# im2col on one core: all plane copies on VectorE, and loads without a descriptor limit

## The chip, the cores and the metric

The kernel runs on 1 core of one Trainium2 chip. The metric is the device time in microseconds (us) of one execution; lower is better. The time before is a median of three runs.

## The reference

The function is im2col with a 3 x 3 window, no padding and stride 1. The input `x` is float32 of shape (16, 64, 32, 32). For each of the 16 x 64 = 1024 image planes and each of the 9 offsets (ki, kj) of the window, the output holds the 30 x 30 subplane that begins at (ki, kj):

```python
h_out = h - kernel_size + 1          # 30
w_out = w - kernel_size + 1          # 30
cols = np.zeros((batch, c * kernel_size * kernel_size, h_out * w_out), dtype=np.float32)
...
            patch = x[b, :, i:i + kernel_size, j:j + kernel_size].copy()
            cols[b, :, col_idx] = patch.ravel()
```

There is no arithmetic in it. 4.19 MB are read, and nine shifted copies of nearly each plane, 33.18 MB, are written.

## The kernel before

The 1024 planes are spread over 128 partitions, 8 planes on each (`CPP` = 8). In DRAM the 8 planes of a partition are 32 KB in one piece (`x_v`), and the 72 output planes that come of them are one piece too (`out_v`). So each load and each store moves, for each of 128 partitions, one long row.

The whole input fits in one buffer, `in_tile`. It is loaded in three pieces, all issued from SyncE's queue (SP) by the helper `load` (L33 to L39): image rows 0 to 32 (plane 0, 4 KB per partition), rows 32 to 200 (the `bulk`, 21 KB per partition) and rows 200 to 256 (7 KB per partition). The helper passes `max_dma_last_dim=7168`, which cuts a row longer than 7168 bytes into descriptors of that size: the bulk becomes 3 descriptors for each partition. The other two loads have rows of 4096 and 7168 bytes and stay whole.

Output planes are built in `out_tile`, which holds two input planes' worth of output (2 x 9 x 900 floats per partition) and has two buffers. The loop at L49 goes over c = 0, 2, 4, 6. For each of the two planes (`s`) and each offset (`kk`) one instruction copies a 30 x 30 window, strided in `in_tile`, to 900 contiguous elements of `out_tile`; that makes 72 copies. The tuple `on_act` (L47) deals them out in turn: of every five copies the second and the fourth go to ScalarE (L57), the rest to VectorE (L59), in all 29 and 43.

Stores are issued from SP too, in the order of the loop. For c = 0 there is one store per plane (L62, 32400 bytes per partition each); for c = 2, 4 and 6 one store per pair of planes (L77, 64800 bytes per partition each). The first store is made to wait, besides its copies, for the bulk load (the manual dependency at L68). As `out_tile` has two buffers, the copies of c = 4 wait until both stores of c = 0 have landed, and those of c = 6 until the store of c = 2 has. The order on each engine is the order of the code (`manual_schedule`). After compilation the first load is moved into the program's first block, ahead of the opening barrier (L94 to L107).

Of the kernel before, what the change touches and what calls it, by code (L numbers as in the profile page):

```python
# [1 line left out]

# [3 lines left out]


def _im2col(ctx, tc, x, K, out):


    nc = tc.nc
    P = nc.NUM_PARTITIONS

    B, C, H, W = x.shape
    HO = H - K + 1
    WO = W - K + 1
    KK = K * K
    assert out.shape == (B, C * KK, HO * WO)
    CPP = B * C // P
    assert CPP * P == B * C and C % CPP == 0 and CPP % 4 == 0  # L20

    x_v = x.rearrange("b (cp c2) h w -> (b cp) (c2 h w)", c2=CPP)
    out_v = out.rearrange("b (cp c2 kk) n -> (b cp) c2 (kk n)", c2=CPP, kk=KK)

    in_pool = ctx.enter_context(tc.tile_pool(name="in_pool", bufs=1))
    out_pool = ctx.enter_context(tc.tile_pool(name="out_pool", bufs=2))

    ctx.enter_context(tc.manual_schedule())

    in_tile = in_pool.tile([P, CPP, H, W], x.dtype, name="in_tile")  # L30
    in_flat = in_tile.rearrange("p c h w -> p (c h w)")

    def load(queue, r0, r1):  # L33

        return queue.dma_start(
            out=in_flat[:, r0 * W : r1 * W],
            in_=x_v[:, r0 * W : r1 * W],
            max_dma_last_dim=7168,
        )  # L39

    cuts = [0, H, 200, CPP * H]
    first = load(nc.sync, cuts[0], cuts[1])
    bulk = load(nc.sync, cuts[1], cuts[2])
    load(nc.sync, cuts[2], cuts[3])


    on_act = (False, True, False, True, False)  # L47
    n = 0
    for c in range(0, CPP, 2):  # L49
        out_tile = out_pool.tile([P, 2, KK, HO, WO], x.dtype, name="out_tile")  # L50
        for s in range(2):
            for kk in range(KK):
                ki, kj = divmod(kk, K)
                src = in_tile[:, c + s, ki : ki + HO, kj : kj + WO]
                dst = out_tile[:, s, kk]
                if on_act[n % len(on_act)]:
                    nc.scalar.copy(out=dst, in_=src)  # L57
                else:
                    nc.vector.tensor_copy(out=dst, in_=src)  # L59
                n += 1  # L60
            if c == 0:
                st = nc.sync.dma_start(  # L62
                    out=out_v[:, s],
                    in_=out_tile[:, s].rearrange("p kk i j -> p (kk i j)"),
                )
                if s == 0:

                    tc.add_manual_dep(  # L68
                        st.ins,
                        bulk.ins.name,  # L70
                        mybir.DependencyInfo(
                            mybir.DependencyClass.Sync, mybir.DependencyReason.DATA
                        ),
                        reason="the store follows the bulk of the loads",
                    )
        if c > 0:
            nc.sync.dma_start(  # L77
                out=out_v[:, c : c + 2].rearrange("p c n -> p (c n)"),
                in_=out_tile.rearrange("p c kk i j -> p (c kk i j)"),
            )  # L80
    return first


def kernel(
    tc: tile.TileContext,
    x: bass.AP,
    kernel_size: bass.AP,
    out: bass.AP,
):
    with ExitStack() as ctx:  # L90
        first = _im2col(ctx, tc, x, int(kernel_size), out)


    tc.close()  # L94
    tc.compile()  # L95
    blocks = tc.nc.main_func.blocks
    load = first.ins
    home = next(b for b in blocks if any(i.name == load.name for i in b.instructions))
    home.instructions = [i for i in home.instructions if i.name != load.name]
    head = list(blocks[0].instructions)  # L100
    at = next(
        k
        for k, i in enumerate(head)
        if i.engine == load.engine and type(i).__name__ == "InstDrain"
    )
    head.insert(at, load)
    blocks[0].instructions = head  # L107


# [1 line left out]
_INS = ['x', 'kernel_size']  # L111
_OUTS = [((16, 576, 900), 'float32')]

_NUMBERS = {'kernel_size': 3}


# [26 lines left out]
```

## Time and profile before

| what | value |
|---|---|
| median of three runs | 91.66 us (91.61 to 92.06) |
| the profiled execution's own time | 91.61 us |
| its span, first to last instruction | 89.8 us |
| VectorE (DVE) busy | 23.5 us, 43 copies |
| ScalarE (ACT) busy | 26.2 us, 29 copies and one table load |
| DMA | 1408 packets, 37.37 MB, busy for 97.2% of 16 engines' span |
| HBM read, written | 4.19 MB, 33.18 MB |

The profile is of one execution. Busy time of an engine is the time in which at least one of its instructions is recorded as running, so overlapping records count once. A DMA packet is one descriptor's work on one of the core's 16 DMA engines. In the answers by stretches of time a packet's bytes and time are put down to the stretch in which it began; so over a stretch shorter than some packets the DMA share can read above 1, and 0 in the next. TensorE has no work here.

### The profile page before, as it was taken

The numbers are of one execution on the slowest core, as the hardware profiler recorded it, in microseconds if no ns is written. First come the engines' busy times: TensorE is split into PE (matmuls) and PEld (weight loads), VectorE is DVE, ScalarE is ACT, GpSimd is POOL, SyncE is SP. The second block draws the span as 40 slices with busy tenths as digits, with TensorE's granted clock in tenths as the row PEclk, the third lists the DMA queues.
The fourth block names the chain that finished last, engine by engine and source line by source line (L and its number), as shares of the span: only waits on it lengthen the run. The fifth ranks groups of instructions, "written<-read, shape, count | busy, mean of one in ns | idle before, by whom it ended". The sixth has DMA issues, their size and how long they took to land.

```text
span 89.8 us, 140 instructions
## 1 busy us (share of the span) xinstructions
DVE 23.5 (26%) x43; ACT 26.2 (29%) x30; POOL 0.2 (0%) x4
## 2 busy tenths in 40 slices
DVE  0380499960000089500000399300000000000000
ACT  5391499930000089910000399300000000000000
POOL 0000000000000000000000000000000000000000
DMA  4999999998899999875999999999999997689990
GB/s 106 428 440 425 418 513 462 462 447 375 361 433 462 693 462 462 375 317 260 433 462 462 462 462 462 462 462 462 462 462 462 462 404 317 289 375 462 462 462 0
DMA packets 1408, 37.37 MB, mean 416 GB/s; under 512 B 128, under 2 KB 128, under 8 KB 768
## 3 DMA queue, kind: packets, MB, share of 16 engines
q1 hardware_dynamic: 1408, 37.37, 97.2%
HBM read 4.19 MB, written 33.18 MB: 416 GB/s over the span
## 4 chain that ended last, share of the span: by engine, by line
DMA 45%; DVE 16%; DVEq 1%; issue 0%; SPq 0%
DMA out_dram<-out_tile 35%; DVE out_tile L59 16%; DMA in_tile<-in_x_dram 10%; DVEq L95 1%; DVEq L59 0%; SPq L77 0%
## 5 line engine op out<-in xcount | busy, mean ns | idle before, releaser
L57 ACT COPY out_tile<-in_tile 128x900 f32<-128x900 f32 x29 | 24.9, 939 | 29.9 <-DMA out_dram<-out_tile 25.3
L59 DVE COPY out_tile<-in_tile 128x900 f32<-128x900 f32 x43 | 23.5, 623 | 33.4 <-DMA out_dram<-out_tile 26.0
L57 ACT ACT_TABLE_LOAD x1 | 1.3, 1283 | 0.8 <-PEq L124 0.8
L124 POOL MEMSET const-bfloat16-1.0<- 128x1 bf16 x1 | 0.1, 102 | 0.0
L124 POOL MEMSET const-uint8-127<- 128x1 uint8 x1 | 0.1, 101 | 0.0
L124 POOL MEMSET const-float32-0.0<- 128x1 f32 x1 | 0.1, 99 | 0.2 <-issue 0.2
L124 POOL MEMSET const-float32-1.0<- 128x1 f32 x1 | 0.1, 98 | 0.0
## 6 DMA issues: line engine op xcount, KB each, us to landing
out_dram<-out_tile SPq DMA_DIRECT2D x3, 8100.0 KB, 31.3
out_dram<-out_tile SPq DMA_DIRECT2D x2, 4050.0 KB, 14.9
in_tile<-in_x_dram SPq DMA_DIRECT2D x1, 2688.0 KB, 9.3
in_tile<-in_x_dram SPq DMA_DIRECT2D x1, 896.0 KB, 11.0
in_tile<-in_x_dram SPq DMA_DIRECT2D x1, 512.0 KB, 3.6
```

Source lines behind the costliest of these rows:

```text
L57: nc.scalar.copy(out=dst, in_=src)
L59: nc.vector.tensor_copy(out=dst, in_=src)
L95: tc.compile()
L124: nc = _bacc.Bacc("TRN2", target_bir_lowering=False, num_devices=1)
```

## The change

Two things change. The helper `load` no longer limits the size of a descriptor, so that the bulk load's 21504 bytes per partition need not be cut. And all 72 copies become `nc.vector.tensor_copy`: `on_act` and its counter go, and no instruction of the kernel's own is left on ScalarE. The stores, the cuts of the loads, the buffers and the manual dependency stay as they are.

```diff
     def load(queue, r0, r1):
 
         return queue.dma_start(
-            out=in_flat[:, r0 * W : r1 * W],
-            in_=x_v[:, r0 * W : r1 * W],
-            max_dma_last_dim=7168,
+            out=in_flat[:, r0 * W : r1 * W], in_=x_v[:, r0 * W : r1 * W]
         )
...
-
-    on_act = (False, True, False, True, False)
-    n = 0
     for c in range(0, CPP, 2):
         out_tile = out_pool.tile([P, 2, KK, HO, WO], x.dtype, name="out_tile")
         for s in range(2):
             for kk in range(KK):
                 ki, kj = divmod(kk, K)
-                src = in_tile[:, c + s, ki : ki + HO, kj : kj + WO]
-                dst = out_tile[:, s, kk]
-                if on_act[n % len(on_act)]:
-                    nc.scalar.copy(out=dst, in_=src)
-                else:
-                    nc.vector.tensor_copy(out=dst, in_=src)
-                n += 1
+                nc.vector.tensor_copy(
+                    out=out_tile[:, s, kk],
+                    in_=in_tile[:, c + s, ki : ki + HO, kj : kj + WO],
+                )
```

## The prediction

> **What bounds the kernel now.** I read the page's engine totals first, then its DMA part, then the DMA traffic by stretches, and last the timeline. The engine totals and the DMA part:
>
> ```profile
> DVE 23.5 (26%) x43; ACT 26.2 (29%) x30; POOL 0.2 (0%) x4
> ...
> DMA packets 1408, 37.37 MB, mean 416 GB/s; under 512 B 128, under 2 KB 128, under 8 KB 768
> ## 3 DMA queue, kind: packets, MB, share of 16 engines
> q1 hardware_dynamic: 1408, 37.37, 97.2%
> ```
>
> Both copying engines are idle for some 70% of the span; the 16 DMA engines are busy for 97.2% of it. What is left is 2.8% of 89.8 us, 2.5 us, and the next view shows where. It is the traffic by stretches; columns are the stretch, its length, VectorE, ScalarE and GpSimd busy time, TensorE clock, DMA share and GB/s:
>
> ```profile
> 0.50:1.00 0.50, 0.00 (x0) 0.21 (x1) 0.00 (x0) 1.00 0.00 0
> 2.00:9.00 7.00, 2.78 (x5) 3.55 (x5) 0.00 (x0) 1.00 1.02 428
> 12.00:30.00 18.00, 7.37 (x14) 6.67 (x8) 0.00 (x0) 1.00 1.00 432
> 30.50:31.00 0.50, 0.00 (x0) 0.00 (x0) 0.00 (x0) 1.00 3.92 1685
> 32.00:50.00 18.00, 5.18 (x10) 6.54 (x8) 0.00 (x0) 1.00 1.00 432
> 57.00:88.00 31.00, 0.00 (x0) 0.00 (x0) 0.00 (x0) 1.00 1.01 435
> ```
>
> Nothing moves before 1.0 us. From 2 to 9 us, the loads, the rate is 428 GB/s at a share of 1.0; in all stretches of stores it is 432 to 435, whether copies run beside them or not (57 to 88 us has none). The half microsecond at 30.5 holds the start of packets worth 1685 GB/s, which is the 64800-byte rows of the store of c = 2 beginning as the store before ends. So the end is set by bytes: 4.19 MB / 428 GB/s = 9.8 us, 33.18 / 432 = 76.8 us, together 86.6 us; with the 1.0 us before the first packet that is 87.6, and the last 2.2 us of the span are the last landing and the closing barrier. The profiled run took 91.61 us, 1.81 more than its span; the median is 91.66, 0.05 above that run, so I carry results over from the run to the median by adding 0.05.
>
> This is read against the chain of waits, which gives VectorE 16% of the span: that is the store of c = 2 waiting for its copies while earlier stores still keep all DMA engines busy. The chain names who released an instruction, not what the queue was short of.
>
> **The copies.** The timeline has the old schedule:
>
> ```profile
> 3.61 2.78 DVE L59 COPY out_tile<-in_tile 128x900 f32<-128x900 f32 x5 [3.61 <-DMA in_tile<-in_x_dram]
> 10.13 8.54 ACT L57 COPY out_tile<-in_tile 128x900 f32<-128x900 f32 x10 [3.04 <-DMA in_tile<-in_x_dram]
> 10.13 9.23 DVE L59 COPY out_tile<-in_tile 128x900 f32<-128x900 f32 x17 [3.74 <-DMA in_tile<-in_x_dram]
> 10.20 3.67 SPq L62 DMA_DIRECT2D out_dram<-out_tile  x2
> 19.44 37.82 SPq L77 DMA_DIRECT2D out_dram<-out_tile  x3
> 31.71 5.46 DVE L59 COPY out_tile<-in_tile 128x900 f32<-128x900 f32 x10 [12.35 <-DMA out_dram<-out_tile]
> 50.85 6.00 DVE L59 COPY out_tile<-in_tile 128x900 f32<-128x900 f32 x11 [13.67 <-DMA out_dram<-out_tile]
> ```
>
> A VectorE copy is recorded for 622 ns (the median of the 43), but 17 of them take 9.23 us, so one begins every (9.23 - 0.62) / 16 = 0.538 us. N copies in a row take (N - 1) x 0.538 + 0.62. ScalarE's 29 copies move over, each 0.538 us on VectorE where ScalarE spent 0.854 (8.54 / 10). Stage by stage:
>
> - Plane 0: 9 copies from 3.61, 4.93 us, done at 8.54. Its store also waits for the bulk load, which ends at 10.1 and lets it go at 10.20. It is covered by 1.6 us; at no cost. If the bulk landed much earlier than now, this cover would shrink, not the time grow.
> - Plane 1: 9 copies from 10.13, done at 15.06 instead of before 13.9. Behind the first store's issue SP's queue has nothing but this store, which is then issued 1.5 us later. The DMA engines have the last load and 4.15 MB of plane 0's store before it, 9.6 us at 432 from about 12, so to 21. Covered by 5 us.
> - c = 2: no buffer wait, so 27 copies in one run from 10.13, 14.61 us, done at 24.74; its store goes at 24.8 instead of 19.44. The DMA engines turn to it at 30.5. The first load, issued at 0.00, had packets by 1.2 us, so the latest issue without a gap is 30.5 - 1.2 = 29.3. Covered by 4.5 us.
> - c = 4: waits for both stores of c = 0, to 31.71 as now; 18 copies, 9.77 us, to 41.5 instead of 38.6. The store of c = 2 (8.29 MB / 432 = 19.2 us) occupies the engines to 49.8. Covered by 7 us.
> - c = 6: waits for the store of c = 2 to land, 50.85 as now; copies to 60.6 instead of 57. The store of c = 4 runs to 69. Covered by 7 us.
>
> So 14.61 + 4.93 + 2 x 9.77 = 39 us of VectorE work replace 23.5, and none of it reaches the end. Every wait that SP had on ScalarE goes; VectorE's own waits for landings stay. What falls away on ScalarE besides copies is its table load of 1.28 us, from 0.8 to 2.1 us; it lies beneath the first load, which lands at 3.61, so it is worth nothing.
>
> [...] The row is the pace above: 0.538 us from start to start. [...] The trace shows the next copy beginning before the record of the last has ended, so I go by the row.
>
> **The load.** The bulk moves 128 x 21504 bytes = 2.75 MB, at the loads' 428 GB/s 6.43 us. With 128 descriptors of 21504 bytes instead of 384 of 7168 no row of the trace shows it: reads here are of 4096 and 7168 bytes, and rows of 32400 and 64800 are writes to HBM. Bounds from the rows: the fastest full microsecond of loading showed 444 GB/s, the slowest 409, so 6.20 to 6.73 us, a gain of 0.23 or a loss of 0.30. I take the long rows' 432, because descriptor length is what the edit changes: 6.37 us, a gain of 0.06. All later DMA work follows without a gap, so this carries through to the end. SP's issue of the bulk takes 0.39 us of its queue now and lies behind the first load's traffic; fewer descriptors can't make it matter.
>
> **Fixed parts.** An engine without instructions of its own still takes part in the opening and closing barriers, so I put nothing down. From above, if a fifth of the 1.81 us outside the span went with ScalarE's work, that is 0.36 us of gain; I see nothing there that could grow.
>
> Sum: 91.61 - 0.06 + 0 = 91.55 for the profiled run, 91.6 for the median.
>
> **The rivals.**
> 1. *VectorE becomes the bound in the stretch from 10.13 us.* Slower than before. Its place is the store of c = 2; it decides when 27 copies end after 29.3 - 0.05, that is at a pace above (29.25 - 10.13 - 0.62) / 26 = 0.71 us per copy, a third slower than measured. At ScalarE's pace of 0.854 the copies end at 10.13 + 26 x 0.854 + 0.94 = 33.3, 4 us late: 95.6. For it: nothing in the trace has VectorE copying with ScalarE idle. Against it: sharing with ScalarE could only have made the measured pace worse. 4%.
> 2. *Reads by long rows run slower.* Beyond the 409 above nothing here prices it; if the 21504-byte rows ran 10% below the loads' 428, that is 0.64 us more, 92.3. It is beyond 0.5% once they lose 7%. For it: no read of that size is in the trace; against it: writes of 64800 bytes run at least as fast as reads of 7168. 10%.
> 3. *More fixed time goes than I put down*, 0.23 from the load and 0.36 from outside the span: 91.66 - 0.59 = 91.1. For it: one engine fewer has code to run; against it: all that is visible of ScalarE is hidden. 10%.
> 4. *The rows are split all the same*, by a limit that I don't see. The stores' 128 packets each of 64800 bytes speak against it. Then the load is as it was, and the time 91.7. 10%.
>
> **How the numbers follow.** My forecast has 66%; with rival 4 that is 76% within 0.5% of 91.66 (91.2 to 92.1), about what a measurement of this kernel can tell from no change. Faster by more is rival 3, 10%; slower by more are rivals 1 and 2, 14%. The likeliest time is 91.6. The range takes in the load's bounds, 91.4 to 92.0, and below them half of what lies outside the span, to 91.2; above, the spread of the runs before, whose highest was 92.06: 91.2 to 92.1. It leaves out most of rivals 1, 2 and half of 3.
>
> **What would show it.** Right: 72 copies on one line, still 622 ns each, VectorE busy for about 39 us; ScalarE without a copy or a table load; 1152 packets (256 fewer) with 384 under 8 KB; the DMA share at 97% and 432 GB/s in the stretches of stores, with no gap near 30.5, 50 and 69 us; the store of c = 2 issued near 24.8 and its time to landing down from 31 to about 26 us; bulk data landed near 10.0. Wrong: a hole in the DMA traffic before a store (rival 1), a bulk that lands after 10.5 (rival 2), or a difference between time and span other than 1.8 us (rival 3).

## The result and the profile after

The changed kernel takes 92.2 us (median of 6 runs, 92.12 to 92.42) against 91.66 for the kernel before (6 runs, 91.61 to 92.06). The ratio is 1.0057, 95% interval 1.0036 to 1.0078: about 0.5 us slower, just above the end of the range on record, and in a direction that the forecast gave little weight. Single executions, of the kernel before too, take over 1.5% longer than the fastest of the same kernel; all ratios leave them out.

The profiled execution took 92.23 us, its span is 90.5; the kernel before had 91.61 and 89.8. So nearly all of the difference lies within the span. The page of the changed kernel, engine totals and DMA queues:

```profile
DVE 39.1 (43%) x72; POOL 0.2 (0%) x4
...
DMA packets 1153, 37.38 MB, mean 413 GB/s; under 512 B 128, under 2 KB 128, under 8 KB 384
## 3 DMA queue, kind: packets, MB, share of 16 engines
q1 hardware_dynamic: 1152, 37.37, 96.5%
q14 instruction: 1, 0.01, 0.0%
```

The first two lines are what was forecast: 39.1 us on VectorE, 256 packets fewer for the kernel's own transfers, 384 under 8 KB. The last line is new. One packet of 0.01 MB ran on a queue that the page of the kernel before does not have: by the queue's name a piece of an engine's program, fetched in mid-run. It is one packet among 1153, and its share rounds to nothing.

The timeline of the changed kernel says that the copies went where the prediction put them:

```profile
10.44 14.61 DVE L49 COPY out_tile<-in_tile 128x900 f32<-128x900 f32 x27 [2.07 <-DMA in_tile<-in_x_dram]
25.08 36.14 SPq L69 DMA_DIRECT2D out_dram<-out_tile  x3
31.96 9.77 DVE L49 COPY out_tile<-in_tile 128x900 f32<-128x900 f32 x18 [6.91 <-DMA out_dram<-out_tile]
51.09 9.77 DVE L49 COPY out_tile<-in_tile 128x900 f32<-128x900 f32 x18 [9.37 <-DMA out_dram<-out_tile]
```

27 copies take 14.61 us and 18 take 9.77, to the digit the worked-out durations. The store of c = 2 goes at 25.08 instead of 19.44, and no store comes too late, as the DMA traffic by stretches shows (columns: stretch, length, VectorE and GpSimd busy, clock, DMA share, GB/s):

```profile
12.00:30.00 18.00, 13.05 (x25) 0.00 (x0) 1.00 1.00 432
57.00:88.00 31.00, 3.86 (x8) 0.00 (x0) 1.00 1.01 435
```

The mean rates of the stores are the old 432 and 435 GB/s. What the mean hides is that the 16 DMA engines no longer end together. Each ends with one 64800-byte packet. In the kernel before, those last packets begin thus (here ScalarE's column is there too):

```profile
85.60:86.20 0.60, 0.00 (x0) 0.00 (x0) 0.00 (x0) 1.00 4.00 1728
86.20:86.80 0.60, 0.00 (x0) 0.00 (x0) 0.00 (x0) 1.00 0.00 0
```

1728 GB/s over 0.60 us is 1.037 MB, which is 16 packets: all have begun by 86.2. In the changed kernel:

```profile
85.60:86.20 0.60, 0.00 (x0) 0.00 (x0) 1.00 3.24 1404
86.20:86.80 0.60, 0.00 (x0) 0.00 (x0) 1.00 0.75 324
```

1404 x 0.60 is 13 packets; three begin later. The last store waits for the slowest engine, so three late engines out of 16 are enough to delay it. Where one of them lost its time is seen around the instruction packet, the DMA queues in the one microsecond from 57 to 58:

```profile
DMA packets 17, 1.04 MB, mean 1045 GB/s; under 512 B 0, under 2 KB 0, under 8 KB 0
...
q14 instruction: 1, 0.01, 1.9%
```

1.9% of 16 engine-microseconds is 0.30 us on one engine. The single packet records of the trace show it from 57.39 to 57.70, between two 64800-byte packets that took 2.63 and 2.75 us where the others take 2.39 to 2.42. So that engine lost about 0.31 + 0.24 + 0.35 = 0.9 us. It is the one that ended last of all, at 89.14 us; the two other late ones ended at 88.77 and 88.74 and came late out of the loads; the slowest engine of the kernel before ended at 88.52. The difference of 0.62 us between 89.14 and 88.52 is the difference between the two profiled times. But the fetch did not make all of it: without its 0.89 us the engine would have ended at 88.25, and the stores with the next one at 88.77. So in this one execution about 0.37 us fall to the fetch and 0.25 to the engines that were late out of the loads, and only runs of each edit alone can say what each is worth.

### The profile page after: what moved, and what is told of

It is laid out like the page before. It is cut to its first block, busy times and chain, and to the rows that moved or that the text cites. A ratio compares the mean times of both kernels' runs of the same rounds, so it can differ in the third digit from the quotient of the medians.

```text
span 90.5 us, 128 instructions
## 1 busy us (share of the span) xinstructions
DVE 39.1 (43%) x72; POOL 0.2 (0%) x4
## 2 busy tenths in 40 slices
DMA packets 1153, 37.38 MB, mean 413 GB/s; under 512 B 128, under 2 KB 128, under 8 KB 384
## 3 DMA queue, kind: packets, MB, share of 16 engines
q1 hardware_dynamic: 1152, 37.37, 96.5%
## 4 chain that ended last, share of the span: by engine, by line
DMA 39%; DVE 26%; DVEq 1%; issue 0%
DMA out_dram<-out_tile 29%; DVE out_tile L49 26%; DMA in_tile<-in_x_dram 11%; DVEq L87 1%; DVEq L49 0%
## 5 line engine op out<-in xcount | busy, mean ns | idle before, releaser
L49 DVE COPY out_tile<-in_tile 128x900 f32<-128x900 f32 x72 | 39.1, 623 | 21.8 <-DMA out_dram<-out_tile 16.3
```

What stands on the lines that cost most here:

```text
L49: nc.vector.tensor_copy(out=out_tile[:, s, kk], in_=in_tile[:, c + s, ki : ki + HO, kj : kj + WO],)
```

## The experiments

The theories at the start were: A, two causes, an instruction fetch that blocks a DMA engine and long read rows that leave some engines late; B, the fetch alone; C, the long rows alone; D, VectorE doing all the copying, or ScalarE being absent. Times are compared by ratios to the kernel before, run beside each.

### The two edits apart

The load edit alone (29 copies stay on ScalarE):

```diff
             in_=x_v[:, r0 * W : r1 * W],
-            max_dma_last_dim=7168,
         )
```

> The kernel before with one edit: no descriptor limit on the loads; 29 copies stay on ScalarE. Theory A (two separate causes: long read rows leave some DMA engines late, and an instruction fetch in mid-run, brought on by VectorE's longer program, blocks one DMA engine): only the first cause is here. In the changed kernel the two slowest engines that the fetch did not touch ended about 0.25 us later than the slowest before, so 91.9 us, and no packet on the instruction queue. Theory B (the fetch alone is the cause, the late engines in that profile were chance): 91.66. Theory C (the long rows cost the whole 0.54 us): 92.2.

Measured: ratio 1.000 (0.998 to 1.0021), median 91.69 us of 12 runs from 91.45 to 92.32. There was no packet on the instruction queue. Its profiled execution, at 91.97 one of the longer ones, shows three of the 16 last packets beginning after 86.2 us, like the changed kernel:

```profile
85.60:86.20 0.60, 0.00 (x0) 0.00 (x0) 0.00 (x0) 1.00 3.24 1404
86.20:86.80 0.60, 0.00 (x0) 0.00 (x0) 0.00 (x0) 1.00 0.75 324
```

So late engines do occur with the long rows, in some executions, but they do not move the median by anything that 12 runs show. C is out, and the half of A that gave the load 0.25 us is wrong as well.

The copies edit alone (all on VectorE, rows cut at 7168 bytes):

```diff
-                if on_act[n % len(on_act)]:
-                    nc.scalar.copy(out=dst, in_=src)
-                else:
-                    nc.vector.tensor_copy(out=dst, in_=src)
-                n += 1
+                nc.vector.tensor_copy(
+                    out=out_tile[:, s, kk],
+                    in_=in_tile[:, c + s, ki : ki + HO, kj : kj + WO],
+                )
```

> The kernel before with the other edit alone: all 72 copies on VectorE, the loads still cut at 7168 bytes. Theory A: one packet of 8 KB on the instruction queue between 50 and 61 us; one engine's stores from there on about 0.89 us late, which makes it the last one by 0.3 to 0.9 us depending on where that engine stood, so 92.0 to 92.5 us. Theory C (long rows alone): 91.66. Theory D (VectorE too slow for a store): a hole in the DMA traffic before the store of c = 2 and over 92.5; the trace of the changed kernel shows none.

Measured: ratio 1.0047 (1.0026 to 1.0068), median 92.12 us. This is the slowdown of the whole change within the intervals, and its page has the packet:

```profile
q1 hardware_dynamic: 1408, 37.37, 96.2%
q14 instruction: 1, 0.01, 0.0%
```

### The same copying with fewer instructions, and more instructions with the same copying

For c > 0 both planes of an offset can be copied by one instruction of 1800 elements. VectorE then does all the copying with 45 instructions:

```diff
+                if c == 0:
                     nc.vector.tensor_copy(
                         out=out_tile[:, s, kk],
                         in_=in_tile[:, c + s, ki : ki + HO, kj : kj + WO],
                     )
+                elif s == 0:
+                    nc.vector.tensor_copy(
+                        out=out_tile[:, :, kk],
+                        in_=in_tile[:, c : c + 2, ki : ki + HO, kj : kj + WO],
+                    )
```

First with the rows cut at 7168 bytes:

> All copies on VectorE, loads cut at 7168 bytes, but for c > 0 one instruction copies both planes of an offset: 45 VectorE copies instead of 72 for the same bytes. Theory A (the number of VectorE instructions brings the fetch on): no packet on the instruction queue in the run, 91.66 like the kernel before. Theory D (it is VectorE doing all the copying, or ScalarE being absent): about as slow as with 72 copies.

Measured: ratio 0.9988 (0.9967 to 1.0009), median 91.67 us. The page of this kernel has no instruction queue, and ScalarE is as idle as in the changed kernel:

```profile
DVE 37.2 (41%) x45; POOL 0.2 (0%) x4
...
q1 hardware_dynamic: 1408, 37.37, 97.3%
```

D is out: VectorE copies everything, for 37.2 us, and the time is that of the kernel before. Then the opposite: ScalarE keeps its 29 copies, and VectorE gets 29 memsets of one element, of no use to the result:

```diff
+    spare = in_pool.tile([P, 1], x.dtype, name="spare")
...
                 n += 1
+                if c > 0 and n > 43:
+                    nc.vector.memset(spare, 0.0)
```

> The kernel before, with ScalarE's 29 copies in place and loads cut, plus 29 one-element memsets on VectorE, so that VectorE runs 72 instructions again without more copying. Theory A: the fetch appears, near the place where VectorE issues its last ones (50 to 57 us), and the time is that of the copies edit alone, 92.0 to 92.5. Theory D: 91.66, as 29 memsets of about 0.06 us are 2 us on an engine with 66 us to spare.

Measured: ratio 1.0045 (1.0028 to 1.0063), median 92.17 us.

```profile
DVE 24.5 (27%) x72; ACT 26.2 (29%) x30; POOL 0.2 (0%) x4
...
q14 instruction: 1, 0.01, 0.0%
```

VectorE's busy time rose by 1.0 us only, on an engine that is idle for over 60 us, and the slowdown is that of the copies edit. It goes with the number of instructions in the program of the engine, not with the work in them.

### How much of it, where, and on which engine

Two fetches, by 157 memsets after VectorE's last copy:

```diff
+    for k in range(157):
+        nc.vector.memset(spare[:, k : k + 1], 0.0)
     return first
```

> The suspected cost doubled: the kernel before plus 157 one-element memsets on VectorE after its last copy, 200 VectorE instructions. [...] Theory A: two packets on the instruction queue; if both hit the same DMA engine 2 x 0.45 us, 92.5; if different ones, one of them sets the end and it is 92.1 to 92.2. If the number of instructions does not matter: one packet and 92.1, or none and 91.7.

Measured: ratio 1.0125 (1.0048 to 1.0202), and two packets:

```profile
DVE 27.3 (30%) x200; ACT 26.2 (29%) x30; POOL 0.2 (0%) x4
...
q14 instruction: 2, 0.02, 0.0%
```

The interval rests on two runs, 92.84 and 93.14, and is too wide to tell two fetches from one. The packet records of the one trace show more. Both fetches ran on the same DMA engine: from the first to the second its packets join end to start. With their longer neighbours they took 0.31 + 0.24 + 0.35 and 0.32 + 0.48, together 1.7 us, and one engine is the last by a wide margin, ending 0.6 us after the next and 1.3 after the third. VectorE was through with everything by 61.4 us, so none of its instructions waits for the second fetch (at 65.3 us). How many instructions one fetch of 8192 bytes holds, no run shows. Among the memsets VectorE pauses once, for 0.32 us at 60.6, and the profile names no cause; whether that is the program running short is open.

The edge, by two single runs. With 17 memsets after the last copy, 60 instructions:

> The kernel before plus 17 one-element memsets on VectorE after its last copy: 60 VectorE instructions. It looks for the point from which the fetch appears. In the three traces that have it, it began when VectorE was starting about its 65th of 72 instructions of the kernel, so Theory A expects none here and the time of the kernel before; if fetches came for any number above 45, one appears at about 57 us.

Measured: a packet on the instruction queue, so the expectation of none was wrong. The time of that one run, 94.51 us, gives the fetch no price: its copies of plane 1 began at 12.78 us instead of 10.13, over 2 us late out of the loads. With 9 memsets, 52 instructions:

> The kernel before plus 9 one-element memsets on VectorE after its last copy: 52 VectorE instructions. 45 had no fetch, 60 had one. [...] One look for the packet on the instruction queue; its time says little.

Measured: no instruction queue on the page, one run of 91.89 us. So the edge for a fetch in mid-run lies between 52 and 60 instructions of the kernel on VectorE. But the trace goes on behind the span of 90.1 us, and there, at 91.25 us, stands the packet that the page does not have; this is the queue between 90 and 93 us:

```profile
q14 instruction: 1, 0.01, 1.2%
```

No other trace has one there. So most likely the same fetch comes at 52 instructions too, only with the closing code, where no store is left to delay, and what counts is how far an engine has come in its program, the code behind the kernel's own included. I had put the edge at 65 from the time at which the packet began; how long before that it was asked for, no trace shows.

The same on ScalarE, by 43 one-element copies after its last copy:

```diff
+    for k in range(43):
+        nc.scalar.copy(out=spare[:, k : k + 1], in_=in_tile[:, 0, 0, 0:1])
     return first
```

> The kernel before plus 43 one-element copies on ScalarE after its last copy: 72 copies on ScalarE, 43 on VectorE as before. It asks whether the fetch belongs to VectorE. If each engine's program is fetched in the same pieces, a packet on the instruction queue appears after about 57 us and the time is 92.1; if it is VectorE's alone, none and 91.7.

Measured: one packet on the instruction queue at 63 us, so ScalarE's program is fetched in the same way. The ratio, 1.0027 (0.9992 to 1.0062), holds both no cost and VectorE's.

An early fetch, by 60 memsets while VectorE waits for the first load:

```diff
+    for k in range(60):
+        nc.vector.memset(spare[:, k : k + 1], 0.0)
     on_act = (False, True, False, True, False)
```

> The kernel before plus 60 one-element memsets on VectorE ahead of its first copy, where VectorE waits for the first load: 103 VectorE instructions. The fetch should then come early, in the loads or the first store, instead of beside 64800-byte packets. If the cost is what the fetch takes on one DMA engine (about 0.3 us recorded, and its neighbours slowed), it is the same or less than in the late place, 91.8 to 92.1, because whatever makes one engine late stays with it to the end. If only a late fetch hurts (Theory F: early delays are made up later), 91.7.

Measured: ratio 1.0077 (1.0061 to 1.0094), median 92.28 us. The timeline, and the queues between 6 and 7 us:

```profile
0.87 1.72 DVE L49 MEMSET spare<- 128x1 f32 x60 [0.87 <-PEq L127]
3.67 2.78 DVE L62 COPY out_tile<-in_tile 128x900 f32<-128x900 f32 x5 [1.08 <-DMA in_tile<-in_x_dram]
```

```profile
q1 hardware_dynamic: 55, 0.39, 97.6%
q14 instruction: 1, 0.01, 1.9%
```

The memsets end a microsecond before the first copy can begin, so they delay no copy. The fetch now falls in the bulk load, 50 us before the place it had, and costs no less; a delay early on was not made up later, and Theory F is out. Whether it costs more than the late one is not shown: the intervals, 1.0061 to 1.0094 and 1.0028 to 1.0063, overlap by a little. Its trace can't price the fetch alone, as in this execution, the longest of the four at 92.48 us, all engines are late (the starts of the last packets, as above):

```profile
85.60:86.20 0.60, 0.00 (x0) 0.00 (x0) 0.00 (x0) 1.00 0.00 0
86.20:86.80 0.60, 0.00 (x0) 0.00 (x0) 0.00 (x0) 1.00 3.74 1620
86.80:87.40 0.60, 0.00 (x0) 0.00 (x0) 0.00 (x0) 1.00 0.25 108
```

Fifteen last packets begin after 86.2, where the kernel before has begun all 16, and one more after 86.8. One 7168-byte packet right behind the fetch took 0.80 us in the records instead of 0.27, but the trace of the copies edit has load packets of up to 0.70 us with no fetch near.

### The version that should beat both

Long rows and 45 VectorE instructions, without ScalarE: the changed kernel less its fetch.

> The changed kernel (long read rows, all copies on VectorE) with one instruction for both planes of an offset where c > 0: 45 VectorE instructions. Theory A as it now stands (the fetch costs the time, the long rows make some engines late in single executions but move the median by nothing that the load edit alone could show, 0.998 to 1.0021): no packet on the instruction queue, 91.7 us, ratio within 0.3% of 1. Theory E (the two edits together cost something that neither costs alone): 92.0 or more.

Measured: ratio 0.9972 (0.9946 to 0.9997), median 91.51 us, no instruction packet. This looked like a gain of 0.26 us, close to the most that the prediction allowed the load, 0.23, so it was run again:

> The kernel with long read rows and 45 VectorE instructions once more, as the version to beat both kernels: it read 0.9972 (0.9946 to 0.9997) against the kernel before, an interval that only just leaves out 1. If the long rows do save the time that fewer descriptors free (0.06 to 0.2 us), again 0.997 to 0.999; if that was the spread of the runs, 1.000 or above.

Measured: ratio 1.0016 (0.9994 to 1.0038), median 91.7 us. The first interval only just left out 1, and the second has it inside; so there is no gain to claim. What stands is that the changed kernel's 0.5 us is gone by both medians; the second interval's upper end, 1.0038, just touches the changed kernel's lower one, 1.0036. Nothing speaks for Theory E, and no version tried here is clearly faster than the kernel before.

## Why the prediction was wrong

- *What bounds the kernel.* Right: bytes at 432 GB/s on 16 engines that are busy throughout (a share of 97.2% before, 96.5% after). I did not draw the consequence. Every DMA engine was busy to the end and the last store waited for the slowest, so a packet of 8192 bytes that took one engine for 0.9 us was on the path, however small it is beside 37 MB.
- *The copies, stage by stage.* Right to a tenth of a microsecond: 4.93, 14.61 and 9.77 us as measured, the stores' issues at 25.08 and 60.9 against 24.8 and 60.6, no hole, all of it covered. The pace of 0.538 us held without ScalarE beside it: 27 copies took 14.61 us.
- *The step that failed* is "29 copies move over, each 0.538 us on VectorE". It counts what the moved instructions do and not that they are 29 more instructions in one engine's program, and so "none of it reaches the end" did not hold. At 72 a fetch of 8192 bytes comes in mid-run, from 57.39 to 57.70 us in the changed kernel's trace, on one of the DMA engines that carry the stores. Its price, left out of the sum altogether, is 0.45% or 0.4 us by the spare instructions (1.0028 to 1.0063), and 0.43 us by the copies edit alone. The kernel before, with 43, lies below the edge, which is between 52 and 60 on VectorE, so its profile had no row for it. VectorE's fetches and ScalarE's both stand under q14. The fetch is hidden from VectorE, whose last 18 copies keep their 9.77 us, but not from the stores.
- *The load.* I gave it a gain of 0.06 us, between 0.23 and a loss of 0.30. The load edit alone measured 1.000 (0.998 to 1.0021), within 0.2 us of nothing either way: the bounds held, and the 0.06 is too small to be told. The bulk landed at 10.42 in the changed kernel's profile instead of the forecast 10.0; with the same long rows and 45 instructions the first store, which waits for it, went at 10.1 in both profiles, as forecast.
- *Fixed parts.* Right: 92.23 - 90.5 is 1.7 us and 91.61 - 89.8 is 1.8. ScalarE's table load and its instructions were worth nothing that shows: without them, and without the fetch, the ratio is 0.9988 (0.9967 to 1.0009).
- *Two readings of the profile before.* The chain's 16% of VectorE are not the store of c = 2 alone: 9.2 us are its copies, and 5.5 us are those of c = 6. And the last 2.2 us of the span are not only a landing and a barrier: the last store packet ends at 88.52, so bytes move until 1.3 us before the end. Neither enters the sum, which starts from the measured 91.61.
- *The rivals.* None of the four happened: VectorE did not become the bound, long rows are not slower by the median, no fixed time went, the rows were not split. The cause was in none of them. The 14% for slower stood for other mechanisms.

The sum as it should have been: 91.66 + 0.4 for the fetch + 0 for the load = 92.1, against 92.2 measured; the 0.1 that is left is inside the interval.

## What to carry to other kernels

Where the DMA engines are busy to the end, count instructions for each engine as well as their time: here VectorE's 72 instructions instead of 43 put one packet of 8192 bytes on one DMA engine in mid-run, and the kernel, whose end is set by the slowest DMA engine, took 0.45% longer. On the page this is one line with a count of 1 and a share of 0.0%, so read the queue list for queues that were not there before, not for shares. If an engine is to take over work, let it do so in fewer and larger instructions where the access pattern allows; here 45 instead of 72 did the same copying at no cost that could be measured.

## What was unexpected of the hardware

- A fetch of 8192 bytes in mid-run cost a saturated kernel 0.45% with the engine that fetched having nothing to wait for; the packet itself is recorded for 0.31 us, its two neighbours on that DMA engine were 0.24 and 0.35 us longer.
- The edge is between 52 and 60 instructions of the kernel on VectorE (at 52 a packet of 8192 bytes comes at 91.25 us, behind the span), the second fetch is there by 200 and ran on the same DMA engine, and ScalarE's program, at 72 copies, was fetched in mid-run too.
- A fetch during the loads cost 0.77% (0.61 to 0.94), no less than one during the stores.
- In some executions one to three DMA engines come out of the loads up to half a microsecond or so behind the rest and stay behind to the end, and in others none. Where two or three did with rows of 21504 bytes (the changed kernel, the load edit), single load packets took up to 1.40 and 1.51 us, with a median of 0.80; in the two profiles with long rows and 45 instructions none took over 1.06. It is not the long rows alone: in the trace of the copies edit, with rows of 7168 bytes, one engine that no fetch touched ended at 89.46, 0.56 us after all others but the fetch's. Nor do the times spread more with the long rows: the 12 runs of the load edit go from 91.45 to 92.32 us, and 28 of the 31 runs of the kernel before beside them from 91.45 to 92.63. What decides this is not settled.
